# A two-part decoder layer on one core: the list scheduler orders the program on the timeline machine model

## The chip, the core and the metric

One core of one Trainium2 chip runs the whole program. The metric is device time in microseconds (us) of one execution; smaller is better. The engines are named as in the profile: PE (TensorE matmul), PEld (its weight loads), DVE (VectorE), ACT (ScalarE), POOL (GpSimd), SP (SyncE, which issues most DMAs here).

## What is computed

One layer with 1024 tokens and width 1024, all in f32:

```python
h = x
h = h + hybrid_mixer(rmsnorm(h), ...)              # SSD heads and stick-breaking attention heads, one projection
h = h + memory_cross_attention(rmsnorm(h), mem...) # 4 heads over 256 memory tokens
h = h + sqrelu_mlp(rmsnorm(h), w1, w2)             # square(relu(hn @ w1)) @ w2, 1024 -> 4096 -> 1024
return rmsnorm(h, final_g)
# stick-breaking: A[t,s] = sigmoid(z_ts) * prod_{s<j<t} (1 - sigmoid(z_tj)), 8 heads of 64
```

## The kernel before

Every f32 operand of a large product is split into a high and a low part by `split` (ACT writes the high part, line 106; DVE subtracts for the low part, line 109), and `mm3` (lines 207 to 209) makes three matmuls of 128 x 128 x 512 out of one. A weight block comes by `piece`: an SP DMA into `wst` (line 190), ACT writes `whi`, DVE writes `wlo`. `whi` and `wlo` have six buffers each, so a block can be prepared only when the PE has finished with an older one.

The stages, in the order of the program: the input and convolution, the projections of the SSD part, and the SSD recurrence with projections woven in (to about 230 us). Then `attention` over 8 heads, about 230 to 525 us. Per head and row block it does a product `z` (line 735), a sigmoid on ACT, a running product `stay` on DVE (`tensor_tensor_scan`, line 738), transposes `wT` on the PE (line 755), a split, and the products `ops` (line 769). The generators of `attention` are interleaved by hand with other products that need nothing from it: the rest of the query, key and value projections (`qkps`, `vps`), the memory's keys and values (`mkv`) and the first half of the output projection (`o` from `yS`). These are called the fillers below. Queries, keys and values go through DRAM (`qd`, `kd`, `vd`) and come back by POOL's DMA queue. After attention come the second half of the output projection and the cross attention (525 to 660 us), the residual, norm and transposes `hT` that feed the MLP (660 to 740 us), the first MLP product (16 blocks of seven products `P1` to `P7`, 740 to about 1040 us), and the second one (`prod2`: 28 products `pr` of 96 matmuls each, to the end), with the final norm at the tail.

Nothing in the kernel fixes the order of instructions on an engine by itself. Each instruction carries a priority number, which grows in the order in which the program is written. `later(by)` shifts it for what stands inside it:

```python
def later(by):
    tc.cur_priority += by
    yield
    tc.cur_priority -= by
```

`piece`, the MLP's weight loads and `both` (the operands of `prod2`) stand in `later(-EARLY)` with `EARLY = 3000`; the evacuations of the projections in `later(-EV)`, `EV = 100`; the split of `wT` in `later(-WP)`, `WP = 60`. When the `TileContext` closes, a list scheduler runs the whole program once against a model of the machine. At each point in the model's time it hands an engine, of the instructions whose inputs and buffers the model has ready, the one that is first by priority. The order that comes out is the order on the chip: each engine takes its instructions one after the other, and waits at the head when its inputs are late. Which of several tiles gets a free buffer (tiles with the same `tag` share `bufs` buffers) is settled on the same run.

## Time and profile before

| what | us |
|---|---|
| median of 3 runs | 1384.64 (1383.60, 1384.64, and one of 2826.73) |
| the profiled execution, its own time | 1381.92 |
| its span, first to last instruction | 1380.2 |
| around the span | 1.7 |

The program has 18343 instructions: 6469 matmuls with as many weight loads, 1521 instructions on DVE, 1304 on ACT, 238 on POOL. A busy time of the PE counts overlapping matmuls once, so a mean duration of 397 ns for one matmul is longer than the distance from one to the next. The span minus the PE's busy time is the time in which no matmul ran.

### The profile page before, as it was taken

What the parts mean: (1) busy time and instruction counts of PE and PEld (TensorE: products, weight loads), DVE (VectorE), ACT (ScalarE), POOL (GpSimd) and SP (SyncE); (2) the same over time, 40 slices, a digit from 0 to 9 for tenths busy, and PEclk for the clock granted to TensorE, in tenths of its full rate; (3) what the DMA queues carried; (4) which work ended last, traced back from release to release, by engine and by line L of the source; (5) the groups of instructions that cost most, each with busy time, mean ns of one, the idle gap of its engine ahead of it and who ended that gap; (6) DMA issues with size and microseconds to landing.
All of it is one profiled execution on the core that took longest, in us unless ns stands there. A gap on an engine that the chain in (4) does not pass through costs nothing.

```text
span 1380.2 us, 18343 instructions
## 1 busy us (share of the span) xinstructions
PE 1313.0 (95%) x6469; PEld 1065.1 (77%) x6469; DVE 972.9 (70%) x1521; ACT 685.3 (50%) x1304; POOL 235.6 (17%) x238
## 2 busy tenths in 40 slices
PE   9999999899998999999898999999999999999987
PEld 7989977687776778887676888888887888888765
DVE  7748864676789765628789666666659855677896
ACT  7355642565567542626555545554444544444343
POOL 0000002210211010000263323321331000000543
PEclk9999999999999999999998999999999999999999
DMA  6111355842656433111224445444368933633232
GB/s 216 39 62 48 103 152 132 240 117 66 168 162 203 132 108 104 47 31 31 92 77 146 167 153 168 131 144 153 130 208 297 320 113 92 236 92 94 75 124 90
DMA packets 95852, 181.68 MB, mean 132 GB/s; under 512 B 9808, under 2 KB 14992, under 8 KB 95760
## 3 DMA queue, kind: packets, MB, share of 16 engines
q1 hardware_dynamic: 85184, 156.04, 35.3%
q0 software_dynamic: 8624, 18.88, 4.9%
q10 hardware_dynamic: 1952, 5.58, 1.1%
q8 instruction: 51, 0.84, 0.2%
q14 instruction: 41, 0.34, 0.1%
HBM read 128.00 MB, written 52.46 MB: 131 GB/s over the span
## 4 chain that ended last, share of the span: by engine, by line
PE 72%; DVE 12%; issue 6%; ACT 4%; DMA 3%; POOL 2%; POOLq 0%; SPq 0%; DVEq 0%; ACTq 0%
PE P L207 7%; PE P L209 7%; PE P L208 7%; PE pr L207 6%; PE pr L208 6%; PE pr L209 6%; DVE stay L738 3%; DVE wlo L109 3%; PE o L209 2%; PE o L207 2%; PE o L208 2%; DMA wst<-in_wp 2%; PE ops L769 1%; PE wT L755 1%; PE qkps L207 1%
## 5 line engine op out<-in xcount | busy, mean ns | idle before, releaser
L208 PE MATMUL pr<-wlo,whi 128*128 128x512 f32 x448 | 177.7, 397 | 11.4 <-DVE wlo L109 11.3
L207 PE MATMUL pr<-whi 128*128 128x512 f32 x448 | 176.4, 396 | 0.7 <-ACT whi L106 0.7
L209 PE MATMUL pr<-whi,wlo 128*128 128x512 f32 x448 | 177.0, 395 | 0.0
L109 POOL TENSOR_TENSOR c<-c 128x512 f32<-128x512 f32 x64 | 88.9, 1400 | 247.6 <-ACT c L106 223.8
L208 PEld LDWEIGHTS pr<-wlo,whi 128*128 128x128 f32 x448 | 84.3, 188 | 35.2 <-DVE wlo L109 15.9
L109 DVE TENSOR_TENSOR wlo<-w1r,whi 128x512 fp32r<-128x512 f32 x92 | 80.7, 878 | 39.9 <-ACT whi L106 39.7
L106 ACT ACTIVATE whi<-w1r 128x512 fp32r<-128x512 f32 x92 | 58.0, 631 | 94.6 <-PE P L208 62.6
L207 PE MATMUL P<-T,whi 128*128 128x512 f32 x256 | 101.6, 397 | 2.0 <-ACT T L106 2.0
L209 PE MATMUL P<-T,wlo 128*128 128x512 f32 x256 | 101.2, 395 | 0.0
L208 PE MATMUL P<-T,whi 128*128 128x512 f32 x256 | 101.0, 394 | 0.0
L207 PEld LDWEIGHTS pr<-whi 128*128 128x128 f32 x448 | 84.3, 188 | 21.1 <-ACT whi L106 1.1
L209 PEld LDWEIGHTS pr<-whi,wlo 128*128 128x128 f32 x448 | 84.3, 188 | 19.7
L106 ACT ACTIVATE c<-c 128x512 f32<-128x512 f32 x128 | 78.7, 628 | 26.4 <-DVE c L109 25.0
L738 DVE TENSOR_TENSOR_SCAN stay<-stay,dg 128x128 f32<-128x128 f32 (+3 forms) x64 | 84.8, 1346 | 3.9 <-ACT stay L106 3.8
L106 ACT ACTIVATE whi<-wst 128x512 fp32r<-128x512 f32 (+1 forms) x88 | 54.1, 628 | 65.3 <-PE o L209 24.6
L106 ACT ACTIVATE whi<-us 128x512 fp32r<-128x512 f32 x64 | 40.3, 629 | 82.9 <-PE pr L208 74.2
L207 PE MATMUL P<-B,whi 128*128 128x512 f32 x192 | 76.8, 400 | 0.0
L208 PE MATMUL P<-B,whi 128*128 128x512 f32 x192 | 76.4, 398 | 0.0
L209 PE MATMUL P<-B,wlo 128*128 128x512 f32 x192 | 76.3, 397 | 0.0
L109 DVE TENSOR_TENSOR wlo<-wst,whi 128x512 fp32r<-128x512 f32 (+1 forms) x88 | 60.5, 705 | 20.8 <-ACT whi L106 20.5
L109 DVE TENSOR_TENSOR wlo<-pair,whi 128x512 fp32r<-128x512 f32 x96 | 74.4, 775 | 0.0
L109 DVE TENSOR_TENSOR wlo<-us,whi 128x512 fp32r<-128x512 f32 x64 | 47.6, 744 | 36.1 <-ACT whi L106 35.9
(332 smaller groups left out, 3425.6 us busy)
## 6 DMA issues: line engine op xcount, KB each, us to landing
ud<-c SPq DMA_DIRECT2D x112, 256.0 KB, 2.5
wst<-in_wp SPq DMA_DIRECT2D x104, 256.0 KB, 2.8
w1r<-in_wp SPq DMA_DIRECT2D x16, 1024.0 KB, 6.4
us<-ud SPq DMA_DIRECT2D x64, 256.0 KB, 2.6
pair<-in_wp SPq DMA_DIRECT2D x16, 1024.0 KB, 6.5
kk<-kd POOLq DMA_DIRECT2D x32, 256.0 KB, 5.1
p<-ud SPq DMA_DIRECT2D x24, 256.0 KB, 2.6
u<-ud SPq DMA_DIRECT2D x24, 256.0 KB, 2.6
```

What stands on the lines that cost most here:

```text
L106: nc.scalar.activation(out=out, in_=in_, func=func, **kw)
L109: (eng or nc.vector).tensor_tensor(out=out, in0=a, in1=b, op=op)
L207: nc.tensor.matmul(out=ps, lhsT=a[0], rhs=b[0], start=start, stop=False)
L208: nc.tensor.matmul(out=ps, lhsT=a[0], rhs=b[1], start=False, stop=False)
L209: nc.tensor.matmul(out=ps, lhsT=a[1], rhs=b[0], start=False, stop=stop)
L738: nc.vector.tensor_tensor_scan(out=stay[:, 0:W][:, ::-1], data0=stay[:, 0:W][:, ::-1], data1=B.dg1[:, S - W:S][:, ::-1], initial=0.0, op0= ...
L755: nc.tensor.transpose(out=t4[:, o:o + P], in_=wb[ii][:, b * P:(b + 1) * P], identity=ident)
L769: nc.tensor.matmul(out=ops[:, oc:oc + 256], lhsT=v, rhs=w[:, sb * 256:sb * 256 + 256], start=(s2_ == 0 and sb == 0 and j == 0), stop=(last ...
```

## The change

One argument of the `TileContext` is set. The list scheduler, the priorities and every instruction stay; the model of the machine on which the order is found becomes the timeline model in place of the default one. The two models differ in what they charge for an instruction, a wait between engines and a DMA, and in how far an engine's queue takes instructions in advance.

```diff
-    with tile.TileContext(nc) as tc:
+    with tile.TileContext(nc, schedule_with_timeline_sim=True) as tc:
         hybrid_trunk(tc, *args, o)
```

## Rows read from the trace of the kernel before

**Rows 1.** The page, busy time of the PE: us, share of the span, instructions.
```profile
PE 1313.0 (95%) x6469; PEld 1065.1 (77%) x6469; DVE 972.9 (70%) x1521; ACT 685.3 (50%) x1304; POOL 235.6 (17%) x238
```
**Rows 2.** The page, the chain that ended last, shares of the span by engine.
```profile
PE 72%; DVE 12%; issue 6%; ACT 4%; DMA 3%; POOL 2%; POOLq 0%; SPq 0%; DVEq 0%; ACTq 0%
```
**Rows 3.** Stretches: us, busy PE, PEld, DVE, ACT, POOL, granted clock, DMA share, GB/s.
```profile
0.00:230.00 230.00, 225.79 (x1332) 191.99 (x1333) 157.44 (x269) 119.26 (x217) 4.70 (x20) 1.00 0.34 104
230.00:525.00 295.00, 269.95 (x1520) 216.29 (x1519) 224.19 (x332) 167.38 (x347) 46.48 (x82) 0.99 0.53 154
525.00:660.00 135.00, 131.84 (x663) 107.41 (x662) 75.13 (x159) 60.24 (x138) 4.62 (x3) 1.00 0.13 40
660.00:740.00 80.00, 67.20 (x320) 53.14 (x318) 63.16 (x100) 44.29 (x87) 39.02 (x33) 0.96 0.30 107
740.00:1290.00 550.00, 547.16 (x2349) 441.70 (x2350) 374.72 (x556) 258.72 (x442) 92.69 (x67) 1.00 0.49 163
1290.00:1380.20 90.20, 71.04 (x292) 54.52 (x291) 78.27 (x110) 35.43 (x76) 48.09 (x34) 0.95 0.29 96
```
**Rows 4.** Waits of the PE from 230 to 525 us: us in total, times, longest.
```profile
PE wT L755 <- DVE stay L738: 15.1, 31, 0.9
PE z L735 <- ACT stay L106: 7.5, 7, 4.9
```
**Rows 5.** The same from 660 to 740 us.
```profile
PE hT L255 <- ACT hn L106: 3.7, 1, 3.7
PE hT L255 <- DVE B L109: 2.9, 2, 1.5
PE hT L255 <- DVE hn L113: 2.2, 2, 1.3
```
**Rows 6.** The same from 1290 us to the end.
```profile
PE pr L208 <- DVE wlo L109: 9.2, 6, 3.2
```
**Rows 7.** The PE's timeline around 256 us (start, us, what), then the stretch behind.
```profile
251.01 0.39 PE L208 MATMUL qkps<-xl,whi 128*128 128x512 f32 x1
256.30 0.69 PE L735 MATMUL z<-kk,qs 128*128 128x384 f32 x1 [4.91 <-ACT stay L106]
...
256.30:262.50 6.20, 6.20 (x18) 4.92 (x19) 4.76 (x8) 4.00 (x9) 0.79 (x1) 0.52 0.77 213
```
**Rows 8.** ACT's timeline: the last evacuation of `ops` of heads 1 and 3.
```profile
283.65 0.59 ACT L106 ACTIVATE oT<-ops 64x512 f32<-64x512 f32 x1
...
331.17 0.60 ACT L106 ACTIVATE oT<-ops 64x512 f32<-64x512 f32 x1 [0.88 <-PE ops L769]
```
**Rows 9.** Groups on the PE from 248 to 512 us, line 207 of each filler.
```profile
L207 PE MATMUL vps<-whi,xh 128*128 128x256 f32 x64 | 18.7, 292 | 0.0
L207 PE MATMUL o<-whi,yS 128*128 128x512 f32 x45 | 18.2, 404 | 0.0
L207 PE MATMUL qkps<-xh,whi 128*128 128x512 f32 x41 | 17.5, 428 | 0.0
L207 PE MATMUL mkv<-whi 128*128 128x512 f32 x32 | 13.0, 408 | 0.0
```
**Rows 10.** A stretch of the second MLP product, matmuls of 512 columns alone.
```profile
1140.00:1180.00 40.00, 40.00 (x174) 32.33 (x173) 23.19 (x37) 16.93 (x30) 0.00 (x0) 1.00 0.34 99
```
**Rows 11.** ACT's and DVE's timelines there: two splits in a row, one accumulation.
```profile
1140.19 0.63 ACT L106 ACTIVATE whi<-us 128x512 fp32r<-128x512 f32 x1 [1.62 <-PE pr L208]
1142.98 0.63 ACT L106 ACTIVATE whi<-p 128x512 fp32r<-128x512 f32 x1 [1.64 <-PE pr L208]
...
1141.46 0.69 DVE L109 TENSOR_TENSOR wlo<-pair,whi 128x512 fp32r<-128x512 f32 x1
1156.01 1.88 DVE L109 TENSOR_TENSOR acc<-acc,pr 128x512 f32<-128x512 f32 x3
```
**Rows 12.** Groups on ACT: loads of its function table.
```profile
L106 ACT ACT_TABLE_LOAD x10 | 12.8, 1283 | 3.5 <-DVE sst L109 2.1 <-PEq L1405 1.3
```
**Rows 13.** The stretch from 1290 to 1345 us.
```profile
1290.00:1345.00 55.00, 45.77 (x185) 34.70 (x185) 54.11 (x70) 22.24 (x47) 36.89 (x24) 0.97 0.32 99
```

## The prediction

> **What bounds the kernel now.** I read the page first: the PE is busy for 1313.0 of 1380.2 us, 95%, and DVE, the next, for 70% [rows 1]. The chain that ended last says the same: 72% of it is the PE, 12% DVE [rows 2]. So a new order, which adds and removes no instruction, can gain at most what the PE now stands idle, 1380.2 - 1313.0 = 67.2 us, while nothing caps what it can lose.
>
> The stretches say where those 67 us are [rows 3]. From 0 to 230 us the PE is idle for 230.0 - 225.8 = 4.2 us; in the attention, 230 to 525 us, for 295.0 - 270.0 = 25.0; from 525 to 660 for 3.2; in the norm before the MLP, 660 to 740, for 12.8; in the MLP, 740 to 1290, for 2.8 of 550; in the tail for 19.2. The reader is to see that two thirds of the program, the projections and the MLP, are closed, and that the order matters in three places: attention, norm, tail.
>
> Then the waits of the PE in these three. In attention it waits 31 times at the head of its queue for the running product of DVE, 15.1 us in total, and 7 times for the sigmoid, 7.5 us, of which one is 4.9 [rows 4]. In the norm it waits for the inputs of `hT`, 3.7 + 2.9 + 2.2 = 8.8 us [rows 5]; in the tail for `wlo`, 9.2 us [rows 6]. These are waits at the head of a fixed order: the model had the input ready at that point, the chip had not. The 4.9 us wait has a price behind it: the stretch from 256.3 to 262.5 us ran at a granted clock of 0.52, which is the 1.2 GHz level, so that 6.2 x (1 - 0.52) = 3.0 us more went [rows 7].
>
> **The change, part by part.** It removes nothing and adds nothing: the same matmuls, splits, DMAs and buffers. What moves is the position of instructions on each engine, DMAs on the SP and POOL queues among them. I can't derive the new order from the trace, so I bound each stretch from both sides.
>
> *0 to 230 and 525 to 660 us.* Below: the idle 4.2 + 3.2 = 7.4 us. Above: the same again, as the PE has ready products behind each other there. I take 0. On ACT the order also sets how often its function table is exchanged, as sigmoids and exponentials of two parts of the program alternate. There are 10 loads of 1.283 us [rows 12]. If each of the 8 chunks of the recurrence caused a further pair, 16 x 1.283 = 20.5 us would come on ACT, which is free for 230.0 - 119.3 = 110.7 us of a stretch that the PE fills [rows 3]. I take 0; if the cover went, it would cost those 20.5.
>
> The Trainium skill, "ScalarE: Activation LUTs", section "What ACT_TABLE_LOAD costs", puts a switch at about 2.66 us with the drain around it; the trace agrees with its load of 1283 ns and shows no drain. By its price 16 switches would be an estimated 42.6 us on ACT, still inside what is free.
>
> *Attention.* Below: all the idle time closed, -25.0 us. Above: the fillers run out before the heads do. Between 248 and 512 us the fillers are 3 x (45 + 41 + 32) = 354 matmuls of 512 columns and 3 x 64 = 192 of 256 [rows 9]. One of 512 takes 40.0 / 174 = 0.230 us [rows 10]; I take half of it, 0.115, for one of 256, hence 81.4 + 22.1 = 103.5 us. The fastest heads end (331.17 - 283.65) / 2 = 23.8 us apart [rows 8], so that 8 heads with no filler between them would take 190. All the fillers in front and the heads alone behind: 103.5 + 190 = 293.5 against 264 now, +30. This extreme needs an order in which every filler overtakes attention; the other needs one in which none is ever missing. The stretch stands at 270 us of PE work in 295 [rows 3], nearer to the closed end, so there is more to lose than to win: I take a third of the way to the loss, +10.
>
> *Norm.* Below: -12.8. Above: its instructions are the same few chains, and a second wait like that of 3.7 us with its slow clock would cost about 7 us; twice that is 14. I take 0.
>
> *The MLP.* Below: -2.8. Above: the operands of `prod2` late. Six `whi` buffers are three pairs; one pair serves 12 matmuls and comes round every 1142.98 - 1140.19 = 2.79 us, and a released buffer is needed two rounds later, 5.58 us. From the start of ACT's split to the end of DVE's second is 1141.46 + 0.69 - 1140.19 = 1.96 us [rows 11], so DVE may be late by 3.6 us. A product with one target puts 4 accumulations of 1.88 / 3 = 0.63 us before them, 2.5 us, which is covered; one with two targets puts 8, 5.0 us, 1.4 late. There are 4 such products: +6. I take 0, as DVE is busy for 374.7 of 550 us and the splits stand at -3000.
>
> *Tail.* Below: the 9.2 us of waits. Above: the same. DVE is busy for 54.1 of the first 55 us [rows 13], so it sets that stretch in any order. I take 0.
>
> Sum against the profiled execution: 1381.9 + 10 = 1391.9. Its own time is 2.7 us below the median of the runs, 1384.6, so on that scale about 1395, +0.7%.
>
> **The rivals.**
>
> *The waits at the head go (faster).* A model that prices latencies nearer to the chip puts ready work in front of the 15.1 + 7.5 + 8.8 + 9.2 = 40.6 us of waits [rows 4 to 6]. For it speaks that in attention fillers exist at that point; against it, that a filler used early is missing later, and that in norm and tail nothing else is ready. Half of the 40.6 with the 3.0 of slow clock: -22, 1363. All of it: -44, 1341.
>
> *The heads run bare (slower).* This is the upper end of attention alone: an engine queue that takes ready instructions far in advance lets fillers pass urgent `z` and `wT`, and the last heads stand alone. The price is +30, 1415. It decides from the point at which more than nine tenths of the fillers have run before the last three heads; for it speaks that the fillers' `later` numbers don't hold them back, only their six weight buffers do.
>
> *The order hardly moves.* Priorities and buffers, not the model's prices, may fix it: 1385. Against it: an order over 18 thousand instructions turns on differences of tens of ns.
>
> **How the numbers follow.** About 2%, 28 us, is what a measurement of this kernel can tell from no change: 1357 to 1412. The likeliest case, a small net loss, 1395 with its own range 1376 to 1412 and a little beyond: chance 0.45, of which 0.05 slower. The waits go: 0.20, half of it under 1357. The bare heads: 0.25, of which 0.23 slower. No movement: 0.10. That makes faster 0.10, same 0.62, slower 0.28. The range reaches from the half-closed waits, 1362, to the bare heads with the MLP's 6 us and one or two new slow-clock stretches of 7 us on top, 1438; I leave 0.09 below it and 0.08 above.
>
> **What would show it.** The counts of instructions stay: 6469 matmuls, 1521 on DVE. The idle time of the PE from 230 to 525 us (or to where attention ends) grows from 25 to some 35 us; if it falls under 15 with fewer than 15 waits of `wT`, the first rival holds. If `qkps`, `vps`, `mkv` and `o` end while heads are left, and those heads come 23 to 24 us apart, the second holds. The MLP should keep its pace of 0.230 us per matmul and under 10 us of idle time. I am wrong in kind if the MLP's stretch grows by more than 10 us, if the SP queue holds a load behind a store that waits, or if the PE's granted clock falls in new places: then the order on an engine that I took for covered reached the PE.

## The result and the profile after

| | before | after |
|---|---|---|
| median of the runs | 1384.7 us | 1428.0 us (1421.1 to 1428.7) |
| ratio | 1 | 1.0304, 95% interval 1.0264 to 1.0344 |
| span of the profiled execution | 1380.2 us | 1427.0 us |
| mean granted clock | 0.991 | 0.967 |

A second measurement of the changed kernel, beside other kernels, gave 1423.5 us, 1.0292 (1.0277 to 1.0308). So it is 3% slower: inside the range given, 1362 to 1438, but the likeliest case (1395) did not come; the slower end did.

The page of the changed kernel, busy times and the shares of the chain that ended last:

```profile
PE 1323.5 (93%) x6469; PEld 1089.4 (76%) x6469; DVE 965.4 (68%) x1521; ACT 684.8 (48%) x1304; POOL 242.4 (17%) x238
...
PE 77%; DVE 9%; DMA 6%; ACT 4%; issue 3%; SPq 1%; POOL 0%; DVEq 0%; ACTq 0%
```

The counts are those of [rows 1]: no instruction on these engines was added or removed (the trace has 18335 instructions in all instead of 18343, a difference in semaphore instructions). The PE's idle time went from 67.2 to 1427.0 - 1323.5 = 103.5 us, 36.3 of the 46.8 us that the span grew. The other 10.5 us are in the PE's busy time. As the matmuls are the same, I put them down to the lower mean clock in the table; no run separates this. In the chain DMA doubled against [rows 2], from 3 to 6%.

To see where, I cut the span at four matmuls that both kernels have: the first `o<-yB` (second half of the output projection), the first `P<-T` (first MLP product), and the first and the last `pr` (second MLP product). The timeline of the PE of the changed kernel, one line for each tile, gives first and last start:

```profile
L207 PE MATMUL o<-whi,yB x64: 387/396/796, 529.8 to 585.4; 128*128 128x512 f32 x64
...
L207 PE MATMUL P<-T,whi x256: 387/393/796, 759.9 to 1061.3; 128*128 128x512 f32 x128
...
L207 PE MATMUL pr<-whi x448: 387/394/796, 1062.0 to 1412.3; 128*128 128x512 f32 x150
```

In the kernel before the same starts are 525.8 for `yB`, 740.0 for the first `P<-T`, 1042.1 and 1369.4 for `pr`. Hence:

| part | before | after | difference |
|---|---|---|---|
| start to first `o<-yB` (projections, attention) | 525.8 | 529.8 | +4.0 |
| to the first `P<-T` (output, cross attention, norm) | 214.2 | 230.1 | +15.9 |
| to the first `pr` (first MLP product) | 302.1 | 302.1 | 0 |
| to the last `pr` (second MLP product) | 327.3 | 350.3 | +23.0 |
| to the end | 10.8 | 14.7 | +3.9 |

A second profiled execution of the changed kernel has 526.5, 226.9, 301.9, 349.9 and 14.8 us for the five parts: the difference of the second part lies between +12.7 and +15.9, those of the last three repeat within 0.4.

The longest wait of the PE, 22.4 us, is about half as long as the loss (22.0 us in the second profile). The PE's waits of the changed kernel (us in total, times, longest), and in a fence of its own its timeline there:

```profile
PE pr L207 <- ACT whi L106: 22.4, 1, 22.4
PE hT L255 <- DVE B L109: 11.8, 4, 5.1
PE pr L208 <- DVE wlo L109: 11.4, 9, 2.6
PE wT L755 <- DVE stay L738: 8.6, 10, 1.7
```

```profile
1069.99 0.50 PE L208 MATMUL pr<-wlo,whi 128*128 128x512 f32 x1 [1.37 <-DVE wlo L109]
1094.50 2.08 PE L207 MATMUL pr<-whi 128*128 128x512 f32 x4 [22.42 <-ACT whi L106]
```

ACT is not the cause: it waited itself, for `us`, the operand that the first product of the second stage reads from DRAM. ACT's timeline, the issues on SP (start, us from the first to the last issue of the line) and a piece of the chain that ended last:

```profile
1093.30 0.63 ACT L106 ACTIVATE whi<-us 128x512 fp32r<-128x512 f32 x1 [25.91 <-DMA us<-ud]
```

```profile
1056.30 2.04 SPq L1294 DMA_DIRECT2D pair<-in_wp  x2
1058.43 3.06 SPq L1156 DMA_DIRECT2D ud<-c  x1
1061.67 8.37 SPq L1294 DMA_DIRECT2D pair<-in_wp  x4
1070.13 3.33 SPq L1305 DMA_DIRECT2D p<-ud  x1
1073.50 0.55 SPq L1305 DMA_DIRECT2D u<-ud  x1
1074.15 3.88 SPq L1226 DMA_DIRECT2D acc<-hd  x2
1078.12 2.45 SPq L1156 DMA_DIRECT2D ud<-c  x1
1080.62 0.55 SPq L1226 DMA_DIRECT2D acc<-hd  x1
1081.26 2.52 SPq L1305 DMA_DIRECT2D us<-ud  x1
```

```profile
1071.18 1.67 DVE pair L109
...
1074.63 3.40 SPq L1226
...
1081.26 11.95 DMA us<-ud
```

A `pair` and an `acc` are 1 MB each, a `us` 0.25 MB. Between 1056 and 1081 us SP issues nine of the large ones, and only then the small one that the PE needs; it lands 11.95 us later. The `acc` issued just ahead of it, at 1080.62, took 11.9 us too: the small load lands when the large ones ahead of it are through. In the kernel before, SP issued `us` loads between single pairs (at 1050, 1052, 1062, 1064, 1071 us), they landed 2.6 to 6.5 us after issue, and the accumulators went out only from 1088 on:

```profile
1050.45 0.32 SPq L1305 DMA_DIRECT2D us<-ud  x1
1050.87 1.56 SPq L1294 DMA_DIRECT2D pair<-in_wp  x1
1052.52 5.73 SPq L1305 DMA_DIRECT2D us<-ud  x2
...
1087.85 0.37 SPq L1226 DMA_DIRECT2D acc<-hd  x1
```

The order on SP is not all that stands on this chain: up to 1072.85 us it runs through DVE, whose work on the pairs SP waits for before it goes on. The stretches of the changed kernel, columns as in [rows 3], show full DMA engines and an idle PE, with the clock falling to 0.58 where it waits and still 0.68 behind:

```profile
1062.00:1072.00 10.00, 8.63 (x37) 6.49 (x35) 9.97 (x17) 3.31 (x7) 5.58 (x1) 1.00 1.05 398
1072.00:1095.00 23.00, 0.58 (x2) 0.50 (x2) 1.88 (x3) 1.15 (x2) 4.48 (x4) 0.58 1.05 392
1095.00:1102.00 7.00, 7.00 (x23) 5.46 (x22) 6.83 (x12) 3.46 (x6) 0.00 (x0) 0.68 0.45 147
```

### The profile page after: what moved, and what is told of

Same layout as the page of the kernel before. It is cut to its first block, busy times and chain, and to the rows that moved or that the text cites. A ratio compares the mean times of both kernels' runs of the same rounds, so it can differ in the third digit from the quotient of the medians.

```text
span 1427.0 us, 18335 instructions
## 1 busy us (share of the span) xinstructions
PE 1323.5 (93%) x6469; PEld 1089.4 (76%) x6469; DVE 965.4 (68%) x1521; ACT 684.8 (48%) x1304; POOL 242.4 (17%) x238
## 4 chain that ended last, share of the span: by engine, by line
PE 77%; DVE 9%; DMA 6%; ACT 4%; issue 3%; SPq 1%; POOL 0%; DVEq 0%; ACTq 0%
PE P L207 7%; PE P L208 7%; PE P L209 7%; PE pr L207 6%; PE pr L208 6%; PE pr L209 6%; DMA wst<-in_wp 3%; DVE wlo L109 2%; PE o L207 2%; PE ops L769 2%; PE o L208 2%; PE qkps L207 2%; PE qkps L209 2%; PE o L209 2%; PE qkps L208 2%
## 5 line engine op out<-in xcount | busy, mean ns | idle before, releaser
L207 PE MATMUL pr<-whi 128*128 128x512 f32 x448 | 124.3, 400 | 22.4 <-ACT whi L106 22.4
L109 POOL TENSOR_TENSOR c<-c 128x512 f32<-128x512 f32 x64 | 94.2, 1483 | 217.2 <-ACT c L106 200.2
L109 DVE TENSOR_TENSOR wlo<-w1r,whi 128x512 fp32r<-128x512 f32 x92 | 76.2, 829 | 48.5 <-ACT whi L106 48.5
L738 DVE TENSOR_TENSOR_SCAN stay<-stay,dg 128x128 f32<-128x128 f32 (+3 forms) x64 | 85.8, 1351 | 13.6 <-ACT stay L106 13.5
L109 DVE TENSOR_TENSOR wlo<-wst,whi 128x512 fp32r<-128x512 f32 (+1 forms) x88 | 61.2, 707 | 22.9 <-ACT whi L106 22.7
```

Of the source, the lines that this page charges most:

```text
L109: (eng or nc.vector).tensor_tensor(out=out, in0=a, in1=b, op=op)
L207: nc.tensor.matmul(out=ps, lhsT=a[0], rhs=b[0], start=start, stop=False)
L738: nc.vector.tensor_tensor_scan(out=stay[:, 0:W][:, ::-1], data0=stay[:, 0:W][:, ::-1], data1=B.dg1[:, S - W:S][:, ::-1], initial=0.0, op0= ...
```

## The experiments

Each time stands as its median and its ratio to the kernel before, measured beside it on the same chip; 0.001 is 1.4 us. Gains over the changed kernel are taken against its second measurement, 1423.5 us and 1.0292. The parts are those of the table above. An edit makes the scheduler order the whole program anew, so I compared the orders in the traces: c1, e1, e2, e7 and e10 leave all but 12 or fewer of the 6469 matmuls at their place, e5 and e8 move some 270 and 290 of them, and e3 and e4 over 1300, with some 300 instructions each on ACT and DVE.

### The loads of the second stage

**e1**, on the changed kernel:

```diff
+    us_dma = []
-    for c, r, n in (...): nc.sync.dma_start(out=c, in_=hd[...])        # 3 accumulators, before the stage
...
-            nc.sync.dma_start(out=w, in_=wp[b_:b_ + 4]...)              # a pair
+            with (tc.issue_after(us_dma[GRP - 1].ins) if g == 1 else ExitStack()):
+                nc.sync.dma_start(out=w, in_=wp[b_:b_ + 4]...)
...
-                    nc.sync.dma_start(out=us, in_=ud[g * GRP + j, UD[which]])
+                    us_dma.append(nc.sync.dma_start(out=us, in_=ud[g * GRP + j, UD[which]]))
...
+            with tc.issue_after(us_dma[GRP - 1].ins):                   # first group, ahead of prod2
+                for c, r, n in (...): nc.sync.dma_start(out=c, in_=hd[...])
```

> The changed kernel with one edit: on the SP queue the weight pairs of the second group (4 loads of 1 MB) and the three loads of the accumulators (1 MB each) are issued only behind the last operand load (us) that the first second-stage products read. Theory A: the 24 us between the first and the last pr matmul come mostly from that order: in the changed kernel 7 MB, some 18 us at its 0.39 MB/us, stand on SP ahead of the first us loads, the PE waits once for 22.4 us, and its clock falls behind it. Then this kernel takes 18 to 24 us less than the changed one: about 1404 to 1410. Rival A2: the DMA engines move all they can there (390 to 400 GB/s), so that whichever load comes first the same bytes are late: 1424 to 1430, with another wait in the place of that of 22.4 us. Either way the attention and the norm stay as they are in the changed kernel.

Measured: 1411.0 us, 1.0218, so 10 us better by the ratios and 12 by the medians. The way from the first to the last `pr` fell from 350.3 to 336.9 us, 13 of the 23. The waits of the PE from 1030 us on in e1:

```profile
PE pr L208 <- DVE wlo L109: 10.3, 9, 2.2
PE pr L207 <- ACT whi L106: 7.3, 3, 3.2
```

The single wait of 22.4 us is gone, and 7.3 in three parts are left. So theory A holds for more than half of the 23 us, and it expected more (18 to 24).

**c1**, the same edit on the kernel before.

> The same edit on the kernel before, as a control. There the us loads already stand among the pair loads, and the accumulators' loads go out at 1088 to 1095 us, well behind the first us. Both theories: 1383 to 1387, no change. If it gains over 5 us, the edit has a value of its own that has nothing to do with the new order, and what e1 gains must be lowered by it.

Measured: 1383.1 us, 0.9999 (0.9989 to 1.0010). The edit is worth nothing where the order was good already.

**e2**, the kernel before with an order of loads like the changed one's, only harsher: all 12 pairs go out before the first `pr`, where the changed kernel has 9 of them and the kernel before 7.

```diff
+                    if load is not None and j == 0 and g == 0:
+                        for j_ in range(GRP): load(j_)                  # 8 pairs, the last also fetches 4 of group 1
...
+                    late_us = g == 0 and load is not None and j >= 4
+                    with ExitStack() as order:
+                        for d in ([held[-1], acc_dma[-1]] if late_us else []):
+                            order.enter_context(tc.issue_after(d.ins))
+                        nc.sync.dma_start(out=us, in_=ud[g * GRP + j, UD[which]])
```

> The kernel before with the order of the changed one put on its SP queue at one place: the first group's pairs as one run, then the four pairs of the second group and the three accumulator loads, and the us loads from the fifth on behind them. PE, DVE and ACT keep the default order. Theory A: a wait of the PE of 10 to 25 us at the first pr matmuls, 1395 to 1410. Rival A2 (the order of those loads makes no odds): 1383 to 1388.

Measured: 1407.9 us, 1.0180 (1.0165 to 1.0195). First `pr` at 1044.0, last at 1395.5: 351.5 us, against 327.3 in the kernel before and 350.3 in the changed one. The compute engines nearly kept the default order, so an order of loads on SP is enough for a loss of this size. That it equals the changed kernel's measures nothing, as the two orders differ (here 11 stores of `c`, too, stand ahead of the accumulators and of the `us` behind them). The PE's waits from 1030 us on, and a stretch:

```profile
PE pr L207 <- ACT whi L106: 22.1, 2, 12.0
```

```profile
1060.00:1080.00 20.00, 7.97 (x24) 5.68 (x24) 5.74 (x8) 1.94 (x5) 1.41 (x1) 0.67 0.92 346
```

**e7** asks whether the place in the queue or the bytes delay `us`. It is the changed kernel with one line different:

```diff
-                    nc.sync.dma_start(out=us, in_=ud[g * GRP + j, UD[which]])
+                    (nc.gpsimd if g == 0 and load is not None else nc.sync).dma_start(out=us, in_=ud[g * GRP + j, UD[which]])
```

> The changed kernel with the 8 operand loads us of the first second-stage product issued on POOL's queue instead of SP's; the weight pairs and the accumulators' loads stay where they are. Theory A in its narrow form: what makes us late is its place behind the other loads in one queue (issued at 1081, some 12 us in flight), so that with a queue of its own it overtakes them: the wait of 22.4 us falls under 8 and the time by 12 to 18 us, 1410 to 1416. Rival A3: the DMA engines work off all outstanding bytes at 390 to 400 GB/s whatever queue they came from, so that us waits for the 7 MB all the same and only an order of issue helps: 1424 to 1432. Rival A4: POOL issues behind its own work, and the wait changes its name: 1420 to 1440.

Measured: 1419.1 us, 1.0258 (1.0239 to 1.0276), 4 to 5 us better. The PE's waits for `whi` from 1030 us on, the timelines of POOL, SP and ACT, and a stretch of e7:

```profile
PE pr L207 <- ACT whi L106: 9.5, 2, 8.7
```

```profile
1071.89 0.56 POOL L1305 DMA_DIRECT2D us<-ud  x1
```

```profile
1091.54 8.71 SPq L1305 DMA_DIRECT2D us<-ud  x3
```

```profile
1077.70 0.63 ACT L106 ACTIVATE whi<-us 128x512 fp32r<-128x512 f32 x1 [9.94 <-DMA us<-ud]
...
1098.55 0.63 ACT L106 ACTIVATE whi<-us 128x512 fp32r<-128x512 f32 x1 [8.79 <-DMA us<-ud]
```

```profile
1070.00:1080.00 10.00, 5.87 (x16) 3.89 (x15) 8.25 (x8) 1.15 (x2) 6.37 (x7) 0.68 1.05 389
```

The load issued on POOL at 1071.89 was used at 1077.70, 5.8 us later, while SP's large loads kept the DMA engines full (389 GB/s). The pairs that SP issued from 1054 to 1066 us took 12.3 to 16.7 us to land, the last of them until 1082.7, so the load from POOL passed them. So a second queue does overtake, against rival A3. But the next product's `us` still came from SP: it went out at 1091.54, and a new wait of 8.7 us stands there. Theory A's mechanism is right and its size was too large: the wait for `whi` fell from 22.4 us to 9.5, not under 8, and part of it came back at the next product. Rival A4 has a share too: the issue at 1071.89 stood behind 7.57 us of POOL's own products `c`, without a gap between them.

The Trainium skill, "DMA: Bandwidth & Descriptors", section "Queues, rings and completion order", says that each DMA engine takes turns between the queues it has work for, packet by packet; the 5.8 us of e7 agree with that.

**e10** tests whether a finer order brings the rest:

```diff
-            with (tc.issue_after(us_dma[GRP - 1].ins) if g == 1 else ExitStack()):
+            with (tc.issue_after(us_dma[GRP + 2 * j].ins) if g == 1 else ExitStack()):
...
-                        load(j)
+                        with (tc.issue_after(us_dma[j - 1].ins) if g == 0 and j else ExitStack()):
+                            load(j)
```

> The edit of e1 carried further: in the first group each pair goes behind the us load of the pair before it, so that pairs and us alternate on SP, and the second group's four pairs are spread behind the us loads of the second product instead of standing together; the accumulators' loads stay behind the first product's last us. In e1 the way from the first to the last pr was 338 us, against 328 in the kernel before and 350 to 352 in the changed one. Theory A in full: these 10 us too are loads in one queue ahead of smaller ones that are needed first; the way falls to 328 to 333 and the time to 1400 to 1405. Rival A5: the 10 us come from the orders on ACT and DVE (and the slow clock behind their waits), which no order of loads mends: 1408 to 1414.

Measured: 1412.8 us, 1.0214; the way of `pr` is 337.3 us, as in e1. The 1400 to 1405 of theory A in full did not come, the 1408 to 1414 of A5 did. The 10 us that stay against 327.3 lie in the first 60 us of the stage, where in e10 one stretch has the DMA engines full, the PE idle and its clock at 0.75:

```profile
1081.60:1101.60 20.00, 12.65 (x36) 9.68 (x37) 9.93 (x17) 7.86 (x15) 0.00 (x0) 0.75 1.05 390
```

That does not prove A5, since the edit did not bring back the order of the kernel before. Only 4 pairs go out before the first `pr` in e10, against 7 there, and the three accumulators stand together. SP's issues, and a piece of the chain that ended last:

```profile
1078.12 4.89 SPq L1319 DMA_DIRECT2D acc<-hd  x3
1084.39 1.12 SPq L1306 DMA_DIRECT2D us<-ud  x1
```

```profile
1084.39 10.68 DMA us<-ud
```

This `us`, right behind three large loads, took 10.68 us, and the PE's longest wait for `whi` in e10 (4.7 us, to 1096.35) ends with it. So large loads ahead of a small one still cost time in e10. How much of the 10 us that makes, and how much the orders on ACT and DVE, no run isolates.

### The fillers of the attention

In the changed kernel the fillers ran ahead: the last `qkps` started at 324 us (before: 395) and the last `o<-yS` at 443 (before: 525). The last heads had the PE to themselves:

```profile
443.00:529.80 86.80, 66.25 (x373) 52.93 (x372) 69.96 (x97) 50.88 (x108) 9.40 (x16) 0.94 0.20 61
```

That is the picture of the rival "the heads run bare", with 20.6 us of idle time in 86.8, but the part is only 4.0 us longer.

**e3**, the kernel before with the fillers in front:

```diff
+    give = [0]
-        with later(GIVE):
+        with later(give[0]):                  # the same in qkps, mkv, o<-yS
...
+    give[0] = -1500                           # from the attention on
```

> The kernel before with the fillers' matmuls (vps, qkps, mkv, o<-yS) given a priority 1500 ahead from the attention on, in the default order otherwise: they run about as early as in the changed kernel, and the last heads run with none left. Theory B, from the trace of the changed kernel: bare heads come 21 us apart and cost only some 4 us, since what the PE stands idle among the last heads it no longer stands idle among the first: 1387 to 1395. Rival B2, the price of the prediction (fillers 103.5 us, then 8 bare heads at 23.8): up to +30, 1400 to 1415.

Measured: 1426.1 us, 1.0312 (1.0296 to 1.0328): +43 us, neither B nor within B2. The first `o<-yB` comes at 564.7 us, +38.9; the part behind it is 6.9 longer, the rest unchanged. Two stretches of e3, and the first of them in the kernel before and in the changed one:

```profile
280.00:320.00 40.00, 38.96 (x242) 34.33 (x241) 11.98 (x21) 14.32 (x32) 0.72 (x1) 1.00 0.47 134
...
451.00:564.70 113.70, 87.94 (x492) 65.55 (x490) 92.89 (x130) 67.55 (x145) 13.93 (x23) 0.95 0.23 65
```

```profile
280.00:320.00 40.00, 37.02 (x262) 32.19 (x260) 32.14 (x47) 26.13 (x59) 4.51 (x7) 1.00 0.31 87
```

```profile
280.00:320.00 40.00, 40.00 (x251) 35.95 (x250) 25.82 (x43) 21.27 (x47) 5.26 (x8) 1.00 0.53 149
```

The fillers ended at much the same time as in the changed kernel (451 against 443 us), with 114 us of bare heads left instead of 87. From 280 to 320 us DVE, which makes the heads' running products, was busy for 12 of 40 us in e3, 32 in the kernel before and 26 in the changed one. My reading is that what costs is how much head work the fillers displaced, rather than when they ended.

**e4**, the changed kernel with the fillers held:

```diff
+    def held():
+        return tc.issue_after(turns[-BACK].ins) if len(turns) >= BACK else ExitStack()    # BACK = 6
-        with later(GIVE):
+        with later(GIVE), held():             # the same in qkps, mkv, o<-yS
...
+                    turns.append(turn)        # the last transpose of each group of wT
```

> The changed kernel with the fillers held back on the PE: each product of vps, qkps, mkv and o<-yS is issued only behind the transposes that stand six groups before it in the program, so that the PE has fillers until the last heads, as in the kernel before. The other engines' orders are left to the new machine. Theory B: the heads that run bare in the changed kernel (443 to 530 us) cost it the 4.0 us by which attention ends later and, through the slow clock of 0.82 behind them, the 5.2 us by which the next stage is longer: together 9 us, so 1415 to 1424 here. Rival B2 (the price of the prediction and of the fillers-first run on the kernel before, +30 to +40, holds in the changed kernel too): 1385 to 1400. Rival B3 (the early fillers also save what they cost, since the PE stands idle less from 230 to 330 us): 1424 to 1432. The second-stage stall stays in all.

Measured: 1435.2 us, 1.0382 (1.0363 to 1.0401), 12 us slower than the changed kernel. `o<-yB` starts at 539.4 instead of 529.8 us. A stretch near the start of the heads, in the changed kernel and in e4:

```profile
230.00:260.00 30.00, 30.00 (x155) 24.89 (x154) 13.71 (x23) 6.96 (x13) 11.37 (x18) 1.00 0.74 206
```

```profile
230.00:260.00 30.00, 23.00 (x102) 18.05 (x101) 11.85 (x20) 6.61 (x12) 11.37 (x18) 0.92 0.74 206
```

Theory B falls here: giving the late heads their fillers back gains nothing, because the early heads then lack them, 7.0 us in this stretch alone. B3 was nearest, and even it expected less loss. The run is no pure test of the fillers, since the scheduler also moved some 290 instructions each on ACT and DVE. My reading is that the plan of the other engines fits the early fillers; no run isolates it.

### The way from the attention to the MLP

Of the +15.9 us, 9.8 are idle time of the PE (25.8 us against 16.0), and 6.1 are longer busy time of the same 977 matmuls, at a mean granted clock of 0.94 against 0.98. About half of it stands at the end, where `P` has begun and the last `hT` transposes wait: from the first `P<-B` to the first `P<-T` 30.5 us, against 22.7 (this stretch of the changed kernel, and the PE's waits in it):

```profile
729.40:759.90 30.50, 19.40 (x83) 14.85 (x81) 25.29 (x35) 17.66 (x33) 19.85 (x15) 0.72 0.29 102
```

```profile
PE hT L255 <- DVE B L109: 7.1, 2, 5.1
PE hT L255 <- ACT hn L106: 2.3, 1, 2.3
```

**e5**, program order on the PE put back on the changed kernel (`xops` is the output product of the cross attention, `hn` the normed row that `hT` transposes, `B` an operand of `P` made from `hT`):

```diff
-                next(units[i - d], None)
+                with behind("xo"):            # behind the last xops matmul so far
+                    next(units[i - d], None)
...
+        with behind("hT"):                    # behind the last hT transpose so far
             for n in range(2):
                 xo_half(t, n)
```

> The changed kernel with program order put back on the PE between the cross attention and the MLP: each half row of xops goes ahead of the cross units behind it, and each row of xops goes behind the hT transposes that precede it in the program. Theory C: of the 10.7 us by which the way from the last o<-yB to the first P<-T is longer in the changed kernel, most comes from transposes that stand behind all of xops and wait for hn and B there: 1417 to 1422, with hT done some 8 us earlier. Rival C2: the transposes wait for DVE, ACT and POOL, whose orders are not touched, and the wait only moves into xops: 1425 to 1432.

Measured: 1430.5 us, 1.0350 (1.0330 to 1.0369), 8 us slower. The waits of the PE from 640 to 761 us in e5:

```profile
PE hT L260 <- DVE hn L113: 9.9, 4, 5.2
PE hT L260 <- DVE B L109: 3.7, 1, 3.7
```

Theory C falls, and the time is C2's. The wait did not move into `xops`, as C2 had it; it changed its name, from `B` to `hn`. From `o<-yB` to `P<-T` it is 234.4 us, and the first MLP product, too, is longer: 306.0 us against 302.1.

**e8** adds the order on POOL, where `nst`, a row's norm factor, had stood behind up to three products `hn`:

```diff
+                with behind("nst") if kh else ExitStack():
                     tt(hn, h[t][:, sl], gff[:, sl], ALU.mult, nc.gpsimd)
```

> The changed kernel with program order on the PE between cross attention and MLP, as in the run that lost 2 to 6 us with it, and in addition the order on POOL: the small nst of a row goes ahead of that row's second hn, as in the kernel before, and no longer behind up to three of them. Theory C3: the first transposes waited for hn, hn on DVE for nst, nst on POOL for hn products of later rows; with both orders put back the way from the last o<-yB to the first P<-T falls from 173.6 us to 165 to 169: 1418 to 1424. Rival C4: the delay comes from the cross attention itself, whose last unit already ends some 8 us late against the stage before, on DVE and ACT: 1426 to 1434.

Measured: 1428.8 us, 1.0339 (1.0315 to 1.0363). From `o<-yB` to `P<-T` 231.7 us, against 234.4 in e5 and 226.9 to 230.1 in the profiles of the changed kernel. C3 falls as well; two engines put in order are not enough. C4, that the cross attention on DVE and ACT is late already, is only left over, not shown.

### Two together, three together

**r1** is the changed kernel once more, **e9** is e1 with e8, **e6** is e1, e4 and e5.

> The changed kernel itself once more, beside the three below, so that each of them is held against it under the same conditions: 1424 to 1432.

> The edits of e1 (SP order of the second stage) and e8 (PE and POOL order of the norm) together on the changed kernel. If both gain as their theories say: 1400 to 1408. If only the SP order gains: 1410 to 1418. In no case does it reach the kernel before, since the rest of the norm, the first products of the second stage and the tail keep some 15 us.

> The changed kernel with all three edits: SP order at the second stage, fillers held, norm order. If the parts add (17 us measured for the first, 9 and 8 expected for the others): 1390 to 1398, and what is left against the kernel before is 7 to 15 us in the first products of the second stage and in the tail. If the better filling of 230 to 330 us in the new order is kept as well: 1380 to 1388, level with the kernel before. If the parts don't add, 1400 to 1411.

Measured: r1 1423.5 us, 1.0292; e9 1419.0, 1.0259; e6 1432.6, 1.0368. The parts add: e9 is 0.0080 below e8, which is the 0.0074 of e1, and e6 is 10.5 us over r1 where the three alone give 12.4 + 8.0 - 10.2 = 10.2. r1 also tells how far profiled executions differ: its `o<-yB` starts at 526.5 us, and in the eight profiles with an untouched attention that start lies between 526.2 and 532.2. The +4.0 of the attention is therefore between 0.4 and 6.4. No version here beats the kernel before.

## Why the prediction came out as it did

The bound on the gain, 67.2 us of idle time, was not put to the test, since a loss came. The steps, one by one:

- *0 to 230 us, taken 0.* Right: the PE is busy for 226.4 us, against 225.8 [rows 3]. The feared table loads did not come; the page's group has the same count and time as [rows 12].

```profile
L106 ACT ACT_TABLE_LOAD x10 | 12.8, 1283 | 3.5 <-DVE sst L109 2.1 <-PEq L1405 1.3
```

- *Attention, taken +10 between -25 and +30.* The sign was right, the size too large: +4.0 (0.4 to 6.4 over the profiles). The sign of the waits was that of the faster rival: `wT` waits for `stay` 8.6 us in 10 waits, not 15.1 in 31 [rows 4]; but the idle time up to `o<-yB` is 27.8 us, not under 15. And the fillers were out before the heads, as the slower rival had it. Both at once nearly cancel. The price of +30 counted fillers and heads one after the other; an order in which fillers displace heads lost still more (e3, +38.9). It does not fit one in which half of the heads run beside them.
- *525 to 660 us and the norm, both taken 0 (up to 7.4 and 14).* Too low: +12.7 to +15.9 together, inside the sum of the bounds. The upper price, waits of a few us with a slow clock behind, is what came: in the first profile idle +9.8 and busy time +6.1. The reason given for 0, that its chains are the same, doesn't carry: the same chains stand in other orders on four engines.
- *The MLP, taken 0, at most +6.* This is the step that failed, and with it the likeliest case. The first product kept its pace, 302.1 us in both. The second grew by 23.0, and the bound was made from ACT's and DVE's splits alone [rows 11]. The prediction names the DMAs on SP's queue among what moves, and the bound counted none: 7 MB of pairs and accumulators that may stand ahead of 0.25 MB, some 18 us at the 0.39 MB per us of the stretch. From the profile before, the second stage's start was visible as the place where SP carries both (in the first 58 us of it the PE is busy for 55.2 and the DMA share is 0.88), and a wait of that size could have been a rival:

```profile
1042.00:1100.00 58.00, 55.20 (x237) 43.78 (x236) 52.40 (x78) 29.56 (x53) 6.31 (x4) 1.00 0.88 295
```

- *Tail, taken 0.* +3.9, within 9.2; `pr` waits for `wlo` 10.0 us there, against 9.2 [rows 6].
- *The signs named.* "Wrong in kind if the MLP's stretch grows by more than 10 us" and "if the granted clock falls in new places" both came. "If the SP queue holds a load behind a store that waits" does not tell the kernels apart: in the 42 us that end 20 us into the second stage, stores at the head of SP waited for ACT and POOL 12.7 us before and 13.5 after. What was new is a load behind loads that are not needed yet.

So the range held, since it took the bare heads with the MLP's 6 us and more slow clock as one case (30 + 6 + 14 on 1384.6 is 1435, not the 1438 given). That case came by its sum, while most of its terms were others: that the time lies inside the range is in good part luck. What e1 shows is the order of loads for 13 of the second stage's 23 us; e2 shows that such an order alone can cost that much. What stays open is the other 10 us there, and the 13 to 16 us between attention and MLP: two partial orders put back did not mend them.

## What to carry over

When an order changes, look first at the queue that carries large loads with slack and small ones without, at the start of a stage: a load that nobody waits for yet can put its duration on the path of the next one in its queue. Cover that is used early need not be lost if the work it covered goes on meanwhile (+4.0 in the changed kernel, +38.9 in e3); compare how much of the critical chain has run when the cover ends, rather than when it ends. And an order is a whole: orders put by hand on the PE (e4, e5) or on PE and POOL (e8) made another plan slower each time, while the queue of loads (e1) could be mended in part alone.

## What the runs showed of the chip

A load of 0.25 MB landed 11.95 us after its issue behind 1 MB loads on the same queue, and was in use 5.8 us after its issue on another queue while the first kept the DMA engines at 389 GB/s; in the kernel before such loads landed 2.6 to 6.5 us after issue (SP, 1041 to 1075 us). The 16 DMA engines moved 387 to 392 GB/s over stretches of 20 us and more (changed kernel, e2, e10). The PE's granted clock fell to 0.58 over the stretch of the 22.4 us wait and was 0.68 in the 7 us behind it, so that part of these still ran at the 1.2 GHz level: 7 x (1 - 0.68) = 2.2 us on top of the wait.
